# Dense blocks of U and V fetched in pairs by one engine, into a pool of their own

## The chip, the cores and the metric

The kernel runs on one core of a Trainium2 chip. The time is the device time of one execution in microseconds (us), and the kernel before stands at the median of three runs. Inside the core, TensorE (PE) multiplies matrices, VectorE (DVE) and ScalarE (ACT) work on rows of data, GpSimd (POOL) does some elementwise work and issues the indexed transfers, and SyncE (SP) issues plain transfers. Transfers between device memory and the on-chip memory are carried by 16 DMA engines, which all issuing engines share.

## The reference, cut to what matters

The program is one inference step of a decoder layer for 336 tokens (16 meta tokens, 256 of a prompt, 64 of running sequences). After convolution, state-space and output projections, every token passes an expert mixer with 16384 experts (PEER). That last part is where the change lies:

```python
q = (xb @ w_q).reshape(T, PEER_HEADS, 2, D_KEY // 2)
s = jnp.einsum('thcd,hckd->thck', q, keys)
s1, i1 = lax.top_k(s[:, :, 0], 16); s2, i2 = lax.top_k(s[:, :, 1], 16)
...
ids = i1 * N_KEYS + i2          # 8 heads x 16 experts per token, out of 16384
g = jax.nn.softmax(sc, axis=-1)
act = gelu(einsum('thkd,td->thk', U[ids], xb))
out = einsum('thk,thkd->td', g * act, V[ids])
```

U and V have 16384 rows of 1024 values each, 64 MB apiece.

## The kernel before, in words

The program is one function, `body`, with nested helpers. Tile's scheduler orders the instructions of each engine from priorities and a timeline of its own; PE's order in the first part is pinned.

**The first 530 us** are the projections, convolutions and state-space parts; weights come through `weight` (line 271) into the pool `wp` (line 290, tiles `wraw` x4, `wh` x2, `wl` x2, 4 KB per partition each).

**The query phase** (the loop over `j` at line 1180) multiplies by `w_q` and scores the keys. In it, `fetch` (line 1173) brings the first eight blocks of U into the pool `pre`.

**The dense phase** serves 184 tokens. U is read as 128 blocks of 128 experts, each block 128 partitions x 1024 floats, 4 KB per partition or 512 KB. `u_block` (line 1410) does 8 matmuls per block (each is two instructions in the trace, so 16 a block) into one of six PSUM tiles, and ACT evicts it with a Gelu into `S` (line 1417). Then V follows as 128 blocks in the same way: `v_block` (line 1514) multiplies `S` by the block into four running sums `va`. Between the blocks, 23 steps in each half (`g_step`, line 1423) build one-hot matrices `oh` on DVE, multiply them on PE into `pg` (line 1443), and scale `S` by the result on DVE (line 1454). So PE, which takes its instructions in order, waits at a step until DVE has built its `oh`.

**The gathered rows** serve the other 136 token columns: `gather` (line 1145) fetches 128 rows of U and V together (8 KB each, 1 MB in all) by an indexed transfer that POOL issues into one of five buffers `wuv`. Each gather is also made to wait for a block some steps back. `pick_dot` (line 1299) takes the products with the token on DVE (line 1303) and passes the sum through two activations on ACT (lines 1305 and 1308, tile `scg`); `pick_sum` (line 1310) adds the scaled V half on DVE (line 1313) and so frees the buffer. Here "row" means one such transfer of 128 rows. `Feed` (line 1350) deals these tasks, and the top-k tasks of the other tokens, out over the dense blocks. All of them go through in-order queues: DVE has top-k, rows and steps in one list, and ACT has evictions, `scg` activations and some transfers in one list.

**How dense blocks are brought**: `bring` (line 1380) issues transfers as long as the ring has room. `ring` (line 1368) hands out tiles `eraw` in the places of `wraw`, `wh` and `wl` of the pool `wp`, eight blocks in all, so block i reuses the place of block i-8. Blocks 8 to 15 take the ring, 16 to 23 go back into the `pre` places, and from 24 on the ring goes round. Line 1398 picks the issuing engine: odd blocks of V, and odd blocks of U after block 24, are issued from ACT, the others from SP. `extra_columns` (line 1287) sends four small transfers (`xigd`) through SP and later reads them back. `residual` reads the stored input `x1d` in two pieces, and `finish` (line 1490) normalizes the gathered tokens, with `fnorm` fetched by SP ahead of it, before `finish_dense` closes the program.

Of the kernel before, what the change touches and what calls it, by code (L numbers as in the profile page):

```python
# [7 lines left out]
F32 = mybir.dt.float32  # L8
# [9 lines left out]
D = 1024  # L18
KD = 8
# [22 lines left out]
ND = T2 - NGAT - NX  # L42
# [20 lines left out]
RB = 4  # L63
RING = RB + 4
LATE = 24
OH = 2
# [92 lines left out]
def body(tc, ia, oa, stop=None):  # L159
    nc = tc.nc  # L160
    with ExitStack() as top:
# [4 lines left out]
        x1d = dr.tile([128, KD, ND], F32, name="x1d")  # L166
        xs, xqs = ExitStack(), ExitStack()
        xq = xqs.enter_context(tc.tile_pool(name="xq", bufs=1, side=RIGHT))
# [120 lines left out]

        wp = top.enter_context(tc.tile_pool(name="wp", bufs=1))  # L290
        mix = top.enter_context(ExitStack())
# [878 lines left out]
        def place_of(n):  # L1170
            return pre_pools[n // PRE].tile([128, D], F32, name="pre", tag=f"pre{n}", bufs=1)

        def fetch(i):
            pre_pools.append(pres[i].enter_context(tc.tile_pool(name=f"pre{i}", bufs=1)))
            for n in range(PRE):
                u = place_of(len(fetched))
                nc.sync.dma_start(u, ia["uT"][len(fetched)])
                fetched.append(u.rearrange("p (k m) -> p k m", k=KD))

        for j in range(16):  # L1180
# [184 lines left out]

        nraw = [0]
# [6 lines left out]
        coming = ([("uT", b) for b in range(2 * PRE, 128)] + [("vE", b) for b in range(XRES)] + [("x1", 0), ("x1", 5)]  # L1373
                  + [("vE", b) for b in range(XRES, 128)])
        landed, turn = {}, [0]

        def again(name, i):
            return name == "uT" and 2 * PRE + RING <= i < AGAIN

        def bring():  # L1380
            while coming:
                name, i = coming[0]
                if again(name, i):
                    if len(ustep) <= i - 2 * PRE - RING:
                        return
                    raw = place_of(i - 2 * PRE - RING)
                else:
                    if turn[0] >= RING + used[0]:
                        return
                    raw = ring()  # L1390
                    turn[0] += 1
                coming.pop(0)
                if name == "x1":
                    n = min(5, KD - i)
                    raw = raw[:, :n * ND].rearrange("p (k t) -> p k t", t=ND)
                    nc.sync.dma_start(raw, x1d[:, i:i + n])
                else:
                    (nc.scalar if i % 2 and (name == "vE" or i > LATE) else nc.sync).dma_start(raw, ia[name][i])
                    raw = raw.rearrange("p (k m) -> p k m", k=KD)
                landed[name, i] = raw  # L1400

        used = [0]

        def block(name, i):
            bring()
            if not again(name, i):
                used[0] += 1
            return landed.pop((name, i))

        def u_block(b):  # L1410
            raw = fetched[b] if b < len(fetched) else block("uT", b)
            tag, nb = (("pj", 3), ("y", 2), ("pj", 3), ("y", 2), ("pj", 3), ("pb", 1))[b % 6]
            p = ps.tile([128, PJ], F32, name="pj", tag=tag, bufs=nb)[:, :T]
            for k in range(KD):
                i_ = nc.tensor.matmul(p[:, :ND], raw[:, k, :], nd[:, k, :], start=(k == 0), stop=(k == KD - 1))  # L1415
            ustep.append(i_.ins.name)
            nc.scalar.activation(Sv(b), p[:, :ND], AF.Gelu)  # L1417
# [62 lines left out]
        def residual():  # L1480
            xr = []
            for k0, n in ((0, 5), (5, 3)):
                r_ = block("x1", k0)
                xr += [r_[:, k] for k in range(n)]
            for k in range(KD):
                nc.tensor.matmul(va[k // 2][:, k % 2], ident, xr[k], start=False, stop=False, skip_group_check=True)
# [72 lines left out]
def layout(i):  # L1559
# [24 lines left out]
    def put(name, a):  # L1584
# [31 lines left out]
        peer_uv=np.concatenate([f["peer_u"][0], f["peer_v"][0]], 1),  # L1616
        uT=f["peer_u"][0].reshape(128, 128, 8, 128).transpose(0, 3, 2, 1).reshape(128, 128, D),
        vE=f["peer_v"][0].reshape(128, 128, D),
        fnorm=f["final_norm_w"],
# [33 lines left out]
```

## Time and profile before

| | |
|---|---|
| median of three runs | 1304.52 us (1301.46 to 1305.58) |
| the profiled execution | 1300.87 us, its span 1299.1 us |
| PE busy | 1270.9 us, 98% of the span |
| DVE, ACT, POOL busy | 74%, 41%, 46% |
| moved by the DMA engines | 373.80 MB |
| mean granted TensorE clock | 0.99 |

How to read the lines of the profile: a page shows one execution. Its slices divide the span into 40 equal parts; a digit is a busy share in tenths, and GB/s is what the DMA engines moved. Groups of instructions have line, engine, operation, `out<-in` by the program's tile names, a count, busy time and the mean of one; then the idle time ahead of them and what ended it. A timeline row has start, length, engine, line, operation, count, and in brackets the idle time before it with what released it. The table by windows has, for each stretch, the busy time of PE, PE's weight loads, DVE, ACT and POOL with their counts, then the granted clock, the DMA engines' busy share and GB/s. In the DMA answers, q0 is the queue of POOL's indexed transfers, q1 the queue of SP and q10 that of ACT.

### The profile page before, as it was taken

Reading aid. Unit: us, or ns where it says so; the run is one execution under the profiler, and the core shown is the slowest. Engines: PE = TensorE matmul, PEld = TensorE weight load, DVE = VectorE, ACT = ScalarE, POOL = GpSimd, SP = SyncE. Lnnn points to the kernel's source line nnn. Section 1 sums busy time; section 2 is a strip of 40 time slices with the busy share of each in tenths; the row PEclk is TensorE's granted clock in tenths of the full one; section 3 lists DMA queues with packets and bytes.
Section 4 is the critical chain, followed back from the end, with each engine's and each line's share of the span. In section 5 each row is a group of like instructions: output and inputs, shape, how many; then the busy total and the mean of one; then the engine's idle time right before and its main releaser. Section 6 shows DMA issues by size and latency. Waiting matters only on the chain.

```text
span 1299.1 us, 23902 instructions
## 1 busy us (share of the span) xinstructions
PE 1270.9 (98%) x9015; PEld 1223.2 (94%) x9015; DVE 956.2 (74%) x2240; ACT 529.6 (41%) x1395; POOL 592.9 (46%) x552
## 2 busy tenths in 40 slices
PE   9999999999989999999999899999999999999997
PEld 7998988999889999999999889999999999999997
DVE  7888778878887235549999968688788888545444
ACT  6787877888766444544232212212110110100102
POOL 2487777877774666974132223223332322122210
PEclk9899999999999999999999989999999999999999
DMA  6435453454433444766989999999999999999992
GB/s 246 165 126 185 155 191 134 156 186 167 149 129 136 146 149 153 254 231 221 382 328 416 416 414 415 414 412 408 413 414 415 415 415 414 402 414 415 405 414 88
DMA packets 85907, 373.80 MB, mean 288 GB/s; under 512 B 10000, under 2 KB 15376, under 8 KB 66208
## 3 DMA queue, kind: packets, MB, share of 16 engines
q1 hardware_dynamic: 48336, 166.82, 34.5%
q0 software_dynamic: 19584, 142.62, 26.9%
q10 hardware_dynamic: 17872, 62.84, 12.1%
q8 instruction: 71, 1.16, 0.4%
q14 instruction: 44, 0.36, 0.1%
HBM read 359.18 MB, written 13.06 MB: 287 GB/s over the span
## 4 chain that ended last, share of the span: by engine, by line
PE 83%; DVE 7%; DMA 6%; ACT 3%; issue 1%; POOL 1%; ACTq 0%; DVEq 0%
PE pj L176 32%; PE va L1517 25%; PE pj L1415 17%; DMA wuv<-in_peer_uv_dram,gid 3%; DMA eraw<-in_uT_dram 3%; PE pg L1443 1%; PE pst L176 1%; DVE ygat L1313 1%; PE po L176 1%; DVE wuv L1303 1%; PE pdec L176 1%; PE psc L1193 1%; PE py L176 1%; DVE pcv L509 1%; DMA wdt<-in_w_dt_dram 1%
## 5 line engine op out<-in xcount | busy, mean ns | idle before, releaser
L1147 POOL DMA_INDIRECT wuv<-in_peer_uv_dram,gid x136 | 173.0, 1272 | 484.7 <-PE va L1517 149.6
L247 POOL TENSOR_TENSOR wl<-wraw,wh 128x1024 fp32r<-128x1024 f32 (+1 forms) x160 | 279.6, 1760 | 117.1 <-ACT wh L243 68.8
L1517 PE MATMUL va<-S,eraw 128*128 128x184 f32 x2048 | 325.4, 320 | 0.0
L1517 PEld LDWEIGHTS va<-S,eraw 128*128 128x128 f32 x2048 | 318.9, 190 | 0.9 <-issue 0.9
L1415 PE MATMUL pj<-nd,eraw 128*128 128x184 f32 x1792 | 294.5, 324 | 9.9 <-DMA eraw<-in_uT_dram 8.1
L1415 PEld LDWEIGHTS pj<-nd,eraw 128*128 128x128 f32 x1792 | 282.8, 192 | 11.3 <-issue 9.0
L1313 DVE SCALAR_TENSOR_TENSOR ygat<-wuv,scg,ygat 128x1024 f32<-128x1024 f32 x128 | 164.1, 1282 | 108.1 <-ACT scg L1308 108.0
L176 PE MATMUL pj<-ah,wh 128*128 128x336 f32 (+1 forms) x768 | 242.5, 326 | 0.3 <-ACT xnf L219 0.3
L176 PE MATMUL pj<-al,wh 128*128 128x336 f32 (+1 forms) x768 | 232.2, 315 | 0.0
L1305 ACT ACTIVATE scg<-scg 128x1 f32<-128x1 f32 x136 | 27.3, 202 | 398.0 <-DVE wuv L1303 220.4
L1303 DVE SCALAR_TENSOR_TENSOR wuv<-wuv,x2m 128x1024 f32<-128x1024 f32 x128 | 156.2, 1220 | 17.3 <-DMA wuv<-in_peer_uv_dram,gid 17.0
L509 DVE SCALAR_TENSOR_TENSOR pcv<-ccat,vec,pcv 128x256 f32<-128x256 f32 x464 | 150.1, 389 | 17.1 <-ACT pcv L507 17.1
L243 ACT CAST wh<-wraw 128x1024 fp32r<-128x1024 f32 x125 | 131.2, 1050 | 73.4 <-PE pj L176 54.0
L176 PEld LDWEIGHTS pj<-ah,wh 128*128 128x128 f32 x768 | 145.4, 190 | 6.3 <-issue 2.0
L176 PEld LDWEIGHTS pj<-al,wh 128*128 128x128 f32 x768 | 145.0, 190 | 0.8
L176 PE MATMUL pj<-ah,wl 128*128 128x336 f32 (+1 forms) x768 | 137.2, 314 | 0.3 <-POOL wl L247 0.3
L176 PEld LDWEIGHTS pj<-ah,wl 128*128 128x128 f32 x768 | 119.8, 188 | 0.7 <-POOL wl L247 0.6
L1417 ACT ACTIVATE S<-pj 128x184 f32<-128x184 f32 x128 | 38.8, 318 | 128.0 <-PE pj L1415 127.7
L523 DVE SCALAR_TENSOR_TENSOR pj<-mcat,vec,pj 128x360 f32<-128x360 f32 x96 | 57.0, 595 | 0.6 <-ACT pj L521 0.6
L1454 DVE SCALAR_TENSOR_TENSOR S<-pg,S 128x232 f32<-128x232 f32 (+1 forms) x92 | 34.7, 420 | 29.8 <-PE pg L1443 29.6
L219 ACT ACT_TABLE_LOAD x38 | 48.8, 1283 | 0.7
L1415 PE MATMUL pj<-nd,pre 128*128 128x184 f32 x256 | 42.0, 319 | 0.0
(387 smaller groups left out, 1694.7 us busy)
## 6 DMA issues: line engine op xcount, KB each, us to landing
wraw<-in_w_in_dram SPq DMA_DIRECT2D x80, 512.0 KB, 3.3
eraw<-in_vE_dram SPq DMA_DIRECT2D x64, 512.0 KB, 9.5
eraw<-in_vE_dram ACTq DMA_DIRECT2D x64, 512.0 KB, 9.4
eraw<-in_uT_dram SPq DMA_DIRECT2D x60, 512.0 KB, 9.2
eraw<-in_uT_dram ACTq DMA_DIRECT2D x52, 512.0 KB, 9.9
st<-in_state_dram SPq DMA_DIRECT2D x8, 1024.0 KB, 6.9
out_ssm_s_dram<-st SPq DMA_DIRECT2D x8, 1024.0 KB, 6.3
wraw<-in_w_mo_dram SPq DMA_DIRECT2D x16, 512.0 KB, 3.2
```

The costliest lines, as they stand in the source:

```text
L176: i_ = nc.tensor.matmul(*a_, **kw)
L219: i_ = nc.scalar.activation(out, in_, f, **kw)
L243: (nc.vector.tensor_copy if on_dve else nc.scalar.copy)(h, src)
L247: (nc.gpsimd if on_pool else nc.vector).tensor_tensor(l[:, q:q + m], src[:, q:q + m], h[:, q:q + m].bitcast(F32), op=OP.subtract)
L509: t = nc.vector.scalar_tensor_tensor(o, i_, wv, a_, op0=OP.mult, op1=OP.add)
L523: nc.vector.scalar_tensor_tensor(o, cat[:, w:w + n], wv, o, op0=OP.mult, op1=OP.add)
L1147: i_ = nc.gpsimd.indirect_dma_start(out=u, out_offset=None, in_=ia["peer_uv"], in_offset=bass.IndirectOffsetOnAxis(ap=gid[:, c:c + 1], axi ...
L1303: nc.vector.scalar_tensor_tensor(u[:, :D], u[:, :D], 1.0, x2m if c < NPICK else x2e, op0=OP.mult, op1=OP.mult, accum_out=w)
L1313: nc.vector.scalar_tensor_tensor(a_, u[:, D:], scg[:, c:c + 1], a_, op0=OP.mult, op1=OP.add)
L1415: i_ = nc.tensor.matmul(p[:, :ND], raw[:, k, :], nd[:, k, :], start=(k == 0), stop=(k == KD - 1))
L1417: nc.scalar.activation(Sv(b), p[:, :ND], AF.Gelu)
L1517: i_ = nc.tensor.matmul(va[k // 2][:, k % 2], raw[:, k, :], Sv(b), start=(b == 0 and k % 2 == 0), stop=(b == 127), skip_group_check=True)
```

## The change

U and V are laid out in pairs of blocks: one transfer brings two blocks, 8 KB per partition, 1 MB. The ring becomes a pool `ep` of four pairs, still 32 KB per partition. It is opened on the right side of the on-chip memory after the query phase, in the place of `wp`, which is moved to the right side and closed there. A pair is free when its second block has been used. All pairs are issued by SP. The `pre` places hold pairs too, the input for `residual` comes in one piece, and the result of `finish` uses a place of `ep`.

```diff
-RING = RB + 4
-LATE = 24
+RING = 4
...
+        wp = wps.enter_context(tc.tile_pool(name="wp", bufs=1, side=RIGHT))
...
         xqs.close()
+        wps.close()
+        ep = top.enter_context(tc.tile_pool(name="ep", bufs=1, side=RIGHT))
...
         def ring():
-            tag, nb = (("wraw", rb[0]), ("wh", 2), ("wraw", rb[0]), ("wl", 2))[nraw[0] % 4]
-            nraw[0] += 1
-            return wp.tile([128, D], F32, name="eraw", tag=tag, bufs=nb)
+            return ep.tile([128, 2 * D], F32, name="eraw", bufs=RING)
...
-                    (nc.scalar if i % 2 and (name == "vE" or i > LATE) else nc.sync).dma_start(raw, ia[name][i])
-                    raw = raw.rearrange("p (k m) -> p k m", k=KD)
-                landed[name, i] = raw
+                    nc.sync.dma_start(raw, ia[name][n])
+                    raw = raw.rearrange("p (a k m) -> p a k m", a=2, k=KD)
+                landed[name, n] = raw
...
+        def block(name, b):
+            raw = pair(name, b // 2)[:, b % 2]
+            if b % 2 == 0:
+                bring()
+            elif not again(name, b // 2):
                 used[0] += 1
+            return raw
...
-            o = [wp.tile([128, D], F32, name="wraw", bufs=rb[0]) for _ in tiles]
+            o_ = ep.tile([128, 2, D], F32, name="o", tag="eraw", bufs=RING)
+            o = [o_[:, a] for a in range(n)]
...
+    def pairs(a):
+        return np.ascontiguousarray(a.reshape(64, 2, 128, D).transpose(0, 2, 1, 3).reshape(64, 128, 2 * D))
...
+        uT=pairs(f["peer_u"][0].reshape(128, 128, 8, 128).transpose(0, 3, 2, 1)),
+        vE=pairs(f["peer_v"][0]),
```

The scheduler writes some engines' lists anew. First SP, from the last `w_q` weights to the reading back of `xigd`. Before:

```order
L1398 DMA eraw<-in_uT_dram 128x1024 x8
L1398 DMA pre<-in_uT_dram 128x1024 x5
L1398 DMA eraw<-in_uT_dram 128x1024 x27
L1292 DMA xigd<-xig 8x8x8 x4
L1398 DMA eraw<-in_uT_dram 128x1024 x8
L1295 DMA xback<-xigd 128x16
```

And now:

```order
L1394 DMA eraw<-in_uT_dram 128x2048 x4
L1394 DMA pre<-in_uT_dram 128x2048 x4
L1394 DMA eraw<-in_uT_dram 128x2048 x26
L1293 DMA xigd<-xig 8x8x8
L1394 DMA eraw<-in_uT_dram 128x2048
L1293 DMA xigd<-xig 8x8x8 x3
L1394 DMA eraw<-in_uT_dram 128x2048 x7
L1296 DMA xback<-xigd 128x16
```

The first four ring transfers stood apart in time before, each behind the part of `wp` that it took over; now the first of them waits for the last use of the whole pool, and the other three follow at once. The small `xigd` transfers stand between pairs, and no dense transfer goes round them on another engine. At the end of the list three pairs stand behind the fetch of `fnorm`, where two single blocks stood.

Second ACT, about block 30 of U, where `scg` is a row's two activations and `S` a block's eviction. Before:

```order
L1417 ACTIVATE S_7584<-pj 128x184
L1398 DMA eraw<-in_uT_dram 128x1024
L1305 ACTIVATE scg<-scg 128x1
L1308 ACTIVATE scg<-scg,ggw 128x1
L1417 ACTIVATE S_7584<-pj 128x184
```

And now, in the same part:

```order
L1418 ACTIVATE S_8020<-pj 128x184 x2
L1306 ACTIVATE scg<-scg 128x1
L1309 ACTIVATE scg<-scg,ggw 128x1
L1418 ACTIVATE S_8020<-pj 128x184 x2
```

No transfer stands in ACT's list any more in the dense phase, and so none behind a row's activations. The place of the rows in the list moves as well. Counted in ACT's list, the rows that stand ahead of a block's eviction are, before and now: block 28 of U, 14 and 9; block 44, 23 and 19; block 72, 39 and 40; block 108, 59 and 61; block 124, 69 and 71.

Third DVE, ahead of the one-hot step that PE takes at block 108. Before, from one step's first matrix to the next:

```order
L1436 TENSOR_TENSOR oh<-iopw,i2T 128x1024
L1437 TENSOR_TENSOR oh<-iopw,i1T 128x512
L1313 SCALAR_TENSOR_TENSOR ygat<-wuv,scg,ygat 128x1024
L1439 TENSOR_TENSOR oh<-oh,gT 128x512 x2
L1303 SCALAR_TENSOR_TENSOR wuv,scg<-wuv,x2m 128x1024
```

And now:

```order
L1437 TENSOR_TENSOR oh<-iopw,i2T 128x1024
L1304 SCALAR_TENSOR_TENSOR wuv,scg<-wuv,x2m 128x1024
L1438 TENSOR_TENSOR oh<-iopw,i1T 128x512
L1440 TENSOR_TENSOR oh<-oh,gT 128x512 x2
L1314 SCALAR_TENSOR_TENSOR ygat<-wuv,scg,ygat 128x1024
L1304 SCALAR_TENSOR_TENSOR wuv,scg<-wuv,x2m 128x1024
L1314 SCALAR_TENSOR_TENSOR ygat<-wuv,scg,ygat 128x1024
L1304 SCALAR_TENSOR_TENSOR wuv,scg<-wuv,x2m 128x1024
L1314 SCALAR_TENSOR_TENSOR ygat<-wuv,scg,ygat 128x1024
L1304 SCALAR_TENSOR_TENSOR wuv,scg<-wuv,x2m 128x1024
L1314 SCALAR_TENSOR_TENSOR ygat<-wuv,scg,ygat 128x1024
```

The steps are the same, but at this place DVE takes four rows between two steps where it took one, so the rows are asked for earlier against the blocks.

More of the change, by code (lines that the diff above doesn't have):

```diff
@@ L166, in body @@
         x1d = dr.tile([128, KD, ND], F32, name="x1d")
-        xs, xqs = ExitStack(), ExitStack()
+        xs, xqs, wps = ExitStack(), ExitStack(), ExitStack()
+        wp = wps.enter_context(tc.tile_pool(name="wp", bufs=1, side=RIGHT))
         xq = xqs.enter_context(tc.tile_pool(name="xq", bufs=1, side=RIGHT))
@@ L1364, in drain, with again @@
                 self.tasks = []
-        nraw = [0]
         def ring():
-            tag, nb = (("wraw", rb[0]), ("wh", 2), ("wraw", rb[0]), ("wl", 2))[nraw[0] % 4]
-            nraw[0] += 1
-            return wp.tile([128, D], F32, name="eraw", tag=tag, bufs=nb)
[L1373 to L1378, printed above, removed]
+            return ep.tile([128, 2 * D], F32, name="eraw", bufs=RING)
+        coming = ([("uT", n) for n in range(PRE, 64)] + [("vE", n) for n in range(XRES // 2)] + [("x1", 0)]
+                  + [("vE", n) for n in range(XRES // 2, 64)])
+        landed, turn, used = {}, [0], [0]
+        def again(name, n):
+            return name == "uT" and PRE + RING <= n < AGAIN // 2
         def bring():
             while coming:
-                name, i = coming[0]
-                if again(name, i):
-                    if len(ustep) <= i - 2 * PRE - RING:
+                name, n = coming[0]
+                if again(name, n):
+                    if len(ustep) < 2 * (n - PRE - RING) + 2:
                         return
-                    raw = place_of(i - 2 * PRE - RING)
+                    raw = place_of(n - PRE - RING)
                 else:
@@ L1393, in bring, with pair @@
                 if name == "x1":
-                    n = min(5, KD - i)
-                    raw = raw[:, :n * ND].rearrange("p (k t) -> p k t", t=ND)
-                    nc.sync.dma_start(raw, x1d[:, i:i + n])
-                else:
-                    (nc.scalar if i % 2 and (name == "vE" or i > LATE) else nc.sync).dma_start(raw, ia[name][i])
-                    raw = raw.rearrange("p (k m) -> p k m", k=KD)
-                landed[name, i] = raw
[L1402 to L1406, printed above, removed]
+                    raw = raw[:, :KD * ND].rearrange("p (k t) -> p k t", t=ND)
+                    nc.sync.dma_start(raw, x1d)
+                else:
+                    nc.sync.dma_start(raw, ia[name][n])
+                    raw = raw.rearrange("p (a k m) -> p a k m", a=2, k=KD)
+                landed[name, n] = raw
+        def pair(name, n):
+            if (name, n) not in landed:
+                bring()
+            return landed[name, n]
+        def block(name, b):
+            raw = pair(name, b // 2)[:, b % 2]
+            if b % 2 == 0:
+                bring()
+            elif not again(name, b // 2):
                 used[0] += 1
-            return landed.pop((name, i))
+            return raw
         def u_block(b):
-            raw = fetched[b] if b < len(fetched) else block("uT", b)
+            raw = fetched[b // 2][:, b % 2] if b < 2 * PRE else block("uT", b)
             tag, nb = (("pj", 3), ("y", 2), ("pj", 3), ("y", 2), ("pj", 3), ("pb", 1))[b % 6]
@@ L1480, in residual @@
         def residual():
[L1481 to L1484, printed above, removed]
+            xr = pair("x1", 0)
+            used[0] += 1
             for k in range(KD):
-                nc.tensor.matmul(va[k // 2][:, k % 2], ident, xr[k], start=False, stop=False, skip_group_check=True)
+                nc.tensor.matmul(va[k // 2][:, k % 2], ident, xr[:, k], start=False, stop=False, skip_group_check=True)
         fin = []
```

9 lines of the change are left out of this document (3 added, 6 removed).

## The prediction, made before the changed kernel was run

> **What bounds the kernel now.** I read the page's chain of waits first, then a table by windows over the dense phase, then PE's timeline where that table shows PE short of busy. The page gives the chain by engine, and what the DMA engines moved in each fortieth of the span:
>
> ```profile
> GB/s 246 165 126 185 155 191 134 156 186 167 149 129 136 146 149 153 254 231 221 382 328 416 416 414 415 414 412 408 413 414 415 415 415 414 402 414 415 405 414 88
> ...
> PE 83%; DVE 7%; DMA 6%; ACT 3%; issue 1%; POOL 1%; ACTq 0%; DVEq 0%
> ```
>
> PE carries the time, but from the middle of the span on the DMA engines stand at about 415 GB/s in nearly every slice. The windows tell which of the two ends last, stage by stage:
>
> ```profile
> 685.00:726.00 41.00, 41.00 (x264) 40.68 (x263) 39.20 (x115) 11.04 (x34) 9.12 (x9) 1.00 1.02 415
> 726.00:779.00 53.00, 45.98 (x284) 44.76 (x282) 39.59 (x82) 12.04 (x47) 13.78 (x12) 0.90 1.02 416
> 779.00:820.00 41.00, 38.13 (x299) 37.36 (x297) 34.78 (x58) 8.69 (x32) 12.18 (x9) 1.00 1.02 416
> 820.00:950.00 130.00, 129.80 (x1045) 127.93 (x1044) 105.21 (x191) 27.53 (x100) 39.79 (x27) 1.00 1.02 412
> 950.00:1118.00 168.00, 168.00 (x1365) 166.59 (x1364) 136.65 (x237) 18.22 (x73) 46.07 (x35) 1.00 1.02 415
> 1118.00:1210.00 92.00, 92.00 (x592) 92.00 (x591) 44.65 (x56) 8.95 (x36) 19.22 (x18) 1.00 1.02 410
> ```
>
> PE is short only between 726 and 820 us, in the U half; over the V half (950 on) it is busy throughout, so nothing in V's transfers can shorten V. The DMA engines' share is 1.02 in all six rows: there is no idle transfer time in the whole stretch. PE's timeline names the losses:
>
> ```profile
> 730.04 5.25 PE L1415 MATMUL pj<-nd,eraw 128*128 128x184 f32 x32 [1.82 <-ACT S L1417]
> 737.40 9.40 PE L1415 MATMUL pj<-nd,eraw 128*128 128x184 f32 x48 [2.10 <-DMA eraw<-in_uT_dram]
> ...
> 773.02 5.25 PE L1415 MATMUL pj<-nd,eraw 128*128 128x184 f32 x16 [3.09 <-DMA eraw<-in_uT_dram]
> ...
> 784.50 7.72 PE L1415 MATMUL pj<-nd,eraw 128*128 128x184 f32 x48
> ...
> 814.54 2.73 PE L1415 MATMUL pj<-nd,eraw 128*128 128x184 f32 x16 [2.87 <-DMA eraw<-in_uT_dram]
> ```
>
> The four waits are 1.82 + 2.10 + 3.09 + 2.87 = 9.88 us. After two of them the granted clock falls (the 0.90 above): 48 instructions take 9.40 us where 48 elsewhere take 7.72, and 16 take 5.25 where 16 take 2.73, so 1.68 + 2.52 = 4.20 more. All that can be won is 14.08 us.
>
> **Why PE waited.** ACT's timeline ahead of the waits, with its own transfers (ACTq) between its work:
>
> ```profile
> 716.91 0.33 ACTq L1398 DMA_DIRECT2D eraw<-in_uT_dram  x1
> ...
> 723.18 0.20 ACT L1305 ACTIVATE scg<-scg 128x1 f32<-128x1 f32 x1 [5.56 <-DVE wuv L1303]
> ...
> 728.02 0.33 ACTq L1398 DMA_DIRECT2D eraw<-in_uT_dram  x1
> ...
> 748.69 0.34 ACTq L1398 DMA_DIRECT2D eraw<-in_uT_dram  x1
> ...
> 762.43 0.20 ACT L1305 ACTIVATE scg<-scg 128x1 f32<-128x1 f32 x1 [4.53 <-DVE wuv L1303]
> 762.44 0.33 ACTq L1398 DMA_DIRECT2D eraw<-in_uT_dram  x1
> ```
>
> ACT's issues stand 11.1 and 13.8 us apart where two blocks take about 5.1 (7.72 us is three blocks): they sit in the list behind a row's activation that waits for DVE. The DMA answers show what this does to the shares. With both dense queues filled (690 to 726 us), and then with one of them only (744 to 748 us):
>
> ```profile
> q0 software_dynamic: 1025, 7.48, 50.6%
> q1 hardware_dynamic: 1015, 3.70, 25.7%
> q10 hardware_dynamic: 1021, 3.70, 25.4%
> ...
> eraw<-in_uT_dram SPq DMA_DIRECT2D x7, 512.0 KB, 10.6
> ```
>
> ```profile
> q0 software_dynamic: 154, 1.11, 66.6%
> q10 hardware_dynamic: 147, 0.54, 33.4%
> ```
>
> The packet counts of the first are equal: the engines give each queue one packet in turn, 8 KB to a row and 4 KB to a block. Two dense queues get half, one gets a third. So a late ACT issue also hands the engines to the rows.
>
> **The change part by part.** *ACT's issues go.* The waits at 737 and 773 us have this cause: 2.10 + 1.68 + 3.09 + 2.52 = 9.39 us. The 1.82 at 730 is an eviction behind a row; the new list has 19 rows ahead of block 44's eviction where there were 23, so I count it as gone too. Upper end 11.21 us. ACT's own saved issue time is worth nothing (ACT is busy 12.04 of 53 us).
>
> *One queue with 8 KB packets.* Against the rows it has turns of equal size: half, as two queues had, and whenever SP has a pair in hand. Neutral while both queues were filled.
>
> *Larger packets.* The page has the cost of both sizes, q0 all rows, q10 mostly blocks:
>
> ```profile
> DMA packets 85907, 373.80 MB, mean 288 GB/s; under 512 B 10000, under 2 KB 15376, under 8 KB 66208
> ...
> q0 software_dynamic: 19584, 142.62, 26.9%
> q10 hardware_dynamic: 17872, 62.84, 12.1%
> ```
>
> Per MB that is 0.269 x 16 x 1299.1 / 142.62 = 39.2 engine-us against 0.121 x 16 x 1299.1 / 62.84 = 40.0: 2% less on the dense half, 1% of the whole, 2.6 us of the 265 from 685 to 950. The Trainium skill ("DMA: Bandwidth & Descriptors", "Anatomy of one DMA") gives a DMA about 2.0 us plus its bytes at 436 GB/s. By that, an estimate, two single blocks cost 6.4 us and a pair 4.4, the engines would cease to bind and the sum would be the upper end. The trace disagrees: with several transfers in flight 415 GB/s were reached with single blocks, so that fixed part is already covered.
>
> *Coarser ring.* A pair is issued when four pairs back is done and needed three pairs later, 6 x 2.57 = 15.4 us. Bounds for its landing: 6.9 us alone, and 16.0 for the median row, of which up to five wait in one queue.
>
> ```profile
> st<-in_state_dram SPq DMA_DIRECT2D x8, 1024.0 KB, 6.9
> ```
>
> I take the 10.6 us above: there too a block was served at 5.05 us (a quarter of 415 GB/s) and a pair at half is the same 5.05. Cover 4.8 us, cost 0; at 16 us it would be 0.6 us per pair.
>
> *xigd.* From 786 to 812 us, blocks behind these small transfers on SP, and on ACT beside them, landed in
>
> ```profile
> eraw<-in_uT_dram SPq DMA_DIRECT2D x5, 512.0 KB, 22.2
> eraw<-in_uT_dram ACTq DMA_DIRECT2D x5, 512.0 KB, 10.6
> ```
>
> SP loses 11.6 us, a turn for each small packet. Now all blocks stand behind them, but a round has one other queue (8 KB) and not two (12 KB): 11.6 x 2/3 = 7.7, less the cover of 4.8 leaves 2.9 us. So the 2.87 at 814 stays.
>
> *Pool behind the query phase.* The ring's first transfers wait for PE's last use of `wp`, which ends just before the first row here; the second row is where the ring's first block is used:
>
> ```profile
> 604.90 0.61 PE L1193 MATMUL psc<-keys,qT 128*128 128x128 f32 x4
> ...
> 619.15 0.79 PE L1415 MATMUL pj<-nd,eraw 128*128 128x184 f32 x4
> ```
>
> 14.2 us for a pair at 10.6: cost 0. The next pairs follow at 5.05 us each and are needed at about 5.1.
>
> *End.* Three pairs stand behind `fnorm` on SP:
>
> ```profile
> 1255.93 0.33 SPq L992 DMA_DIRECT2D wuv<-in_fnorm_dram  x1
> 1260.24 5.31 SPq L1398 DMA_DIRECT2D eraw<-in_vE_dram  x2
> ```
>
> The first of these pairs can be issued when all but 12 blocks are done, about 1257 us, later than 1255.93; cost 0 while rows are not over 5 us late.
>
> *What the engines take back.* With a share of 1.02 up to 950 us and beyond, PE can be at V 11.2 us sooner only if 11.2 x 415 = 4.6 MB are moved sooner or left for later. Cheaper packets give 2.6 us. Rows can be late by what they land early: the median from issue to landing in 690 to 850 and in 850 to 950 us is
>
> ```profile
> q0 software_dynamic: 5012, 36.48, 55.3%
> ...
> wuv<-in_peer_uv_dram,gid POOLq DMA_INDIRECT x34, 16.0
> ```
>
> ```profile
> wuv<-in_peer_uv_dram,gid POOLq DMA_INDIRECT x21, 11.4
> ```
>
> so 4.6 us. But the new order asks for rows earlier late in U: 61 for 59 ahead of block 108's eviction, 71 for 69 at 124; two rows of 1.05 MB are 5.1 us. That leaves 2.6 + 4.6 - 5.1 = 2.1 us as the lower end. Between 2.1 and 11.2 I take 5.0, nearer to the lower end because of the 1.02, and above it because early in U the order asks for fewer rows (9 for 14 at block 28), which frees DVE's early time.
>
> The sum: 1300.87 - 5.0 = 1295.9 us for a profiled execution like this one. The median of the runs shown is 3.65 us above it; from the median, 1304.5 - 5.0 = 1299.5 us.
>
> **The rivals.** *All waits go* (chance 0.18): rows prove less pressing than counted, and PE runs through U. 11.2 us, up to 14.1 with `xigd`: about 1292. For it: the chain to the waits went through ACT. Against: the 1.02.
>
> *The engines bind wholly* (0.20): the waits reappear as PE waiting at `pg` for `oh` or at an eviction. 2.1 us less, or nothing: 1303.
>
> *Rows become late* (0.20), slower. In 690 to 850 us rows had 55.3% of queue time; a punctual dense queue holds them to 50. Then 34 rows become 30.7, 3.3 rows late at 160 / 34 = 4.7 us, 15.5 us. Less the 4.6 they can bear, 10.9; about half of it falls on PE, since a PE that waits fills its ring and then leaves the engines to the rows: 5.5 us slower, 1310. It decides from about 7 us of lateness on, at the steps about block 72 to 110, where DVE takes up to four rows ahead of one `oh`. For it: the new DVE list there. Against: PE's lost time no longer feeds back through ACT's issues.
>
> *One queue gets a third* (0.04): pairs are cut into 4 KB turns, so the change does not do what it says. Dense blocks would get 138 GB/s beside five queued rows, 3.8 us a block; each such spell would cost PE what it lost at 737 and 773 us, and it would come oftener: 6 us slower, 1310. Against: 85907 - 66208 = 19699 packets of 8 KB or more are over 2000 more than the 17408 of 136 rows, so SP's transfers with 8 KB per partition, as `st`, go in whole packets. The Trainium skill ("DMA: Bandwidth & Descriptors", "SWDGE vs HWDGE vs iDMA") states a packet of preferably at most 4096 B as the boundary at which an engine changes queues. By that rule this case holds; the counts here say otherwise.
>
> **How the numbers follow.** The forecast has 0.38 and 1299.5 us. A measurement of this kernel tells 0.3%, 3.9 us, from no change. Faster by more: all of the first rival, most of the forecast's case (0.27), 0.02 of the second: 0.47. Within: 0.10 of the forecast's, 0.15 of the second, 0.03 of the third: 0.28. Slower: 0.25, the rest. The range reaches from 1290 (every wait gone) to 1311 (rows late, with 1 us of spread).
>
> **What would show it.** Right: no wait for `eraw` at PE about blocks 50 to 66, all dense traffic on q1 at near half of the engines' time with packets of 8 KB, the share still 1.02, a wait about block 78 behind `xigd`, V begun about 5 us sooner and unchanged in length. Wrong: a share clearly under 1 between 685 and 950 us (first rival), PE waiting for DVE's `oh` by more than 5 us in sum (second or third), or pairs landing after 15 us away from `xigd`.

## The result, and the profile after

The changed kernel takes 1312.19 us (median of 10 runs, 1308.13 to 1314.76), the kernel before 1304.44 us (10 runs, 1301.46 to 1306.61): a ratio of 1.0058, interval 1.0043 to 1.0072, 7.6 us slower. The profiled execution took 1310.24 us, 9.37 more than the one before the change, its span 1308.5 us.

The page's chain of waits, by engine: PE has lost share, DVE has gained.

```profile
PE 71%; DVE 17%; DMA 6%; ACT 3%; issue 2%; POOL 1%; ACTq 0%; DVEq 0%
```

The table by windows for the stretches that the prediction showed:

```profile
685.00:726.00 41.00, 38.46 (x248) 38.17 (x248) 39.82 (x110) 12.70 (x37) 15.12 (x10) 1.00 1.01 412
726.00:779.00 53.00, 49.47 (x326) 48.86 (x326) 35.34 (x51) 10.16 (x44) 14.94 (x13) 0.97 1.01 419
779.00:820.00 41.00, 35.47 (x259) 34.79 (x258) 31.31 (x52) 7.33 (x32) 12.15 (x10) 0.92 1.01 419
820.00:950.00 130.00, 126.47 (x1025) 125.03 (x1024) 114.38 (x204) 27.32 (x107) 38.36 (x28) 0.99 1.01 416
```

The DMA engines are as full as they were (share 1.01). From 685 to 950 us together they moved 416 GB/s where it was 414: if the larger packets did that, they are worth 0.5%, half of what was taken. PE's timeline has the losses, and they are others:

```profile
719.63 20.21 PE L1416 MATMUL pj<-nd,eraw 128*128 128x184 f32 x128 [2.54 <-ACT S L1418]
...
743.37 6.67 PE L1416 MATMUL pj<-nd,eraw 128*128 128x184 f32 x32 [3.53 <-ACT S L1418]
...
791.70 8.08 PE L1416 MATMUL pj<-nd,eraw 128*128 128x184 f32 x32 [4.94 <-ACT S L1418]
...
811.34 0.76 PE L1444 MATMUL pg<-oh 128*128 128x64 f16 x10 [0.46 <-DVE oh L1440]
...
852.35 1.29 PE L1444 MATMUL pg<-oh 128*128 128x64 f16 x16 [3.39 <-DVE oh L1440]
```

PE no longer waits for a dense block. It waits 14.86 us for evictions and one-hot matrices that stand in ACT's and DVE's lists behind rows, where it waited 9.88 us before. ACT's timeline ahead of the first of these waits shows the order: the row's activation waits for DVE, and the two evictions come right behind it.

```profile
718.84 0.20 ACT L1306 ACTIVATE scg<-scg 128x1 f32<-128x1 f32 x1 [4.34 <-DVE wuv L1304]
719.08 0.29 ACT L1309 ACTIVATE scg<-scg,ggw 128x1 f32<-128x1 f32 x1
719.28 0.52 ACT L1418 ACTIVATE S<-pj 128x184 f32<-128x184 f32 x2
```

Four points of the timeline tell where the 9.37 us come in: the ring's first product (619.15 before), V's first product and the first product of the final normalization, after and then before:

```profile
620.74 0.79 PE L1416 MATMUL pj<-nd,eraw 128*128 128x184 f32 x4
...
957.47 3.00 PE L1517 MATMUL va<-S,eraw 128*128 128x184 f32 x16
...
1294.43 2.63 PE L1530 MATMUL prd<-sqd,cst 128*128 128x184 f32 x14
```

```profile
950.80 2.71 PE L1517 MATMUL va<-S,eraw 128*128 128x184 f32 x16
...
1287.47 2.63 PE L1530 MATMUL prd<-sqd,cst 128*128 128x184 f32 x14
```

Ahead of the ring's first product 1.6 us are lost, in U 5.1 (336.7 for 331.7), in V 0.3, behind V 2.4 (14.1 for 11.6 to the span's end): 9.4 us.

**The 1.6 us** are scatter. In eleven experiments, kernels of both kinds, that product falls between 618.7 and 622.2 us. So from here on the *dense stage* is counted from it to the first `prd` product: 668.3 us before, 673.7 after. (Some expectations below count from block 12, 11.0 us later: 657.3 and 662.6.)

**The 2.4 us behind V** are two table loads of ACT in the last chain:

```profile
1280.46 1.28 ACT L1501 ACT_TABLE_LOAD   x1
1281.75 1.28 ACT L1306 ACT_TABLE_LOAD   x1
...
1298.33 1.28 ACT L219 ACT_TABLE_LOAD   x1 [1.10 <-DVE rsv L233]
1299.63 0.36 ACT L219 ACTIVATE rst<-rsv 128x184 f32<-128x184 f32 x1
1300.00 1.28 ACT L219 ACT_TABLE_LOAD   x1
```

The scheduler now puts the preload for the normalization (L1501) ahead of the last row's Gelu (L1306), which loads its own table over it. Each later function then loads a table again. Before, the preload stood behind the last row and the chain had no load. The Trainium skill ("ScalarE: Activation LUTs", "What ACT_TABLE_LOAD costs") gives a switch 1.28 us and a drain of 1.38 us more. The load agrees; the drain does not show here, since the next activation starts 0.02 us after the load.

**The 5.1 us in U.** What the DMA engines did between 560 and 605 us, before and after:

```profile
DMA packets 2183, 8.00 MB, mean 178 GB/s; under 512 B 240, under 2 KB 240, under 8 KB 2177
...
eraw<-in_uT_dram SPq DMA_DIRECT2D x7, 512.0 KB, 3.2
wraw<-in_w_q_dram SPq DMA_DIRECT2D x5, 512.0 KB, 3.3
pre<-in_uT_dram SPq DMA_DIRECT2D x3, 512.0 KB, 5.1
```

```profile
DMA packets 1027, 3.85 MB, mean 86 GB/s; under 512 B 120, under 2 KB 120, under 8 KB 997
...
wraw<-in_w_q_dram SPq DMA_DIRECT2D x5, 512.0 KB, 3.9
```

The parts of `wp` used to come free one at a time, and ten blocks were issued in these 45 us, while the engines were half idle. The new pool opens when all of `wp` is done, and its first pair is issued at 606.78: 4.15 MB are missing by then. PE does not notice, as the ring is used only from 620.74 on. But the first rows now share the engines with the whole ring: row 5, counted from 0, has its last packet at 648.7 us for 642.3. The scheduler's lists also put the early rows off (9 for 14 at block 28). The bytes moved in the 165 us that end 65.85 us behind the ring's first product, before and after:

```profile
520.00:685.00 165.00, 164.74 (x1111) 163.50 (x1110) 131.07 (x522) 64.78 (x174) 85.75 (x99) 1.00 0.77 286
```

```profile
521.59:686.59 165.00, 164.74 (x1110) 163.43 (x1109) 129.93 (x553) 64.64 (x168) 78.18 (x94) 1.00 0.69 270
```

16 GB/s over 165 us: 2.6 MB are still missing (the rates are whole GB/s, so this and the table's MB are good to about 0.15). What is missing there is rows, not blocks. The queues in the same two stretches, before and after:

```profile
q1 hardware_dynamic: 7963, 26.49, 43.9%
q0 software_dynamic: 2365, 17.28, 27.4%
q10 hardware_dynamic: 859, 3.14, 4.9%
```

```profile
q1 hardware_dynamic: 6233, 30.57, 47.9%
q0 software_dynamic: 1891, 13.79, 20.6%
```

SP and ACT had moved 26.49 + 3.14 = 29.63 MB, now SP alone 30.57: the blocks have caught up. The rows are 3.49 MB behind. Two things hold them back. The engines are full from 635 to 655 us (share 1.01 and 1.02 in the two halves), and DVE's list has top-k work ahead of the rows: row 5 is taken 5.6 us after its landing before the change (647.91), and 12.8 us after it now, with DVE busy in between. So buffers come free later, and the engines even have time left then:

```profile
661.48 1.22 DVE L1304 SCALAR_TENSOR_TENSOR wuv<-wuv,x2m 128x1024 f32<-128x1024 f32 x1
```

```profile
665.00:675.00 10.00, 10.00 (x67) 10.00 (x66) 9.90 (x17) 1.84 (x8) 2.78 (x3) 1.00 0.71 270
```

From 685 us to V the engines are full, and 2.6 MB at 415 GB/s are 6.4 us. This is the theory that the experiments test: **a debt of early transfers**, carried through a stretch in which the engines have nothing to spare. Its rivals are the queues' shares (one queue with 8 KB packets holds the rows to half) and the rows' places in the lists.

### The profile page after: what moved, and what is told of

The parts are those of the page before. It is cut to its first block, busy times and chain, and to the rows that moved or that the text cites. A ratio compares the mean times of both kernels' runs of the same rounds, so it can differ in the third digit from the quotient of the medians.

```text
span 1308.5 us, 23635 instructions
## 1 busy us (share of the span) xinstructions
PE 1271.7 (97%) x9015; PEld 1224.8 (94%) x9015; DVE 959.9 (73%) x2240; ACT 532.1 (41%) x1400; POOL 597.6 (46%) x552
## 4 chain that ended last, share of the span: by engine, by line
PE 71%; DVE 17%; DMA 6%; ACT 3%; issue 2%; POOL 1%; ACTq 0%; DVEq 0%
PE pj L176 31%; PE va L1517 24%; PE pj L1416 7%; DMA wuv<-in_peer_uv_dram,gid 5%; DVE ygat L1314 3%; DVE wuv L1304 3%; PE pg L1444 1%; PE pst L176 1%; PE po L176 1%; PE pdec L176 1%; PE py L176 1%; DVE pcv L508 1%; ACT L219 1%; DVE S L1455 1%; DMA wdt<-in_w_dt_dram 1%
## 5 line engine op out<-in xcount | busy, mean ns | idle before, releaser
L1146 POOL DMA_INDIRECT wuv<-in_peer_uv_dram,gid x136 | 179.3, 1318 | 483.6 <-PE va L1517 164.6
L1306 ACT ACTIVATE scg<-scg 128x1 f32<-128x1 f32 x136 | 27.6, 203 | 472.6 <-DVE wuv L1304 472.5
## 6 DMA issues: line engine op xcount, KB each, us to landing
eraw<-in_uT_dram SPq DMA_DIRECT2D x56, 1024.0 KB, 10.2
```

Of the source, the lines that this page charges most:

```text
L1146: i_ = nc.gpsimd.indirect_dma_start(out=u, out_offset=None, in_=ia["peer_uv"], in_offset=bass.IndirectOffsetOnAxis(ap=gid[:, c:c + 1], axi ...
```

## The experiments

All numbers in one table. The ratio is to executions of the kernel before on the same chip; the medians come from several chips, so runs are compared by their ratios. The dense stage is that of one profiled execution. "Missing" is the difference in MB to the kernel before in those 165 us.

| run | median us | ratio (95%) | dense stage us | missing MB |
|---|---|---|---|---|
| before | 1304.44 | 1 | 668.3 | 0 |
| after | 1312.19 | 1.0058 (1.0043 to 1.0072) | 673.7 | 2.6 |
| e1_tail | 1310.65 | 1.0044 (1.0028 to 1.0061) | 676.0 | 2.6 |
| e2_late | 1306.70 | 1.0016 (1.0001 to 1.0031) | 673.6 | 3.1 |
| e3_sp | 1302.30 | 0.9987 (0.9972 to 1.0002) | 668.3 | -0.5 |
| e4_raw | 1308.41 | 1.0040 (1.0025 to 1.0054) | 676.4 | 1.8 |
| e5_early | 1307.29 | 1.0015 (1.0004 to 1.0026) | 673.3 | 1.5 |
| e6_skip | 1307.55 | 1.0017 (1.0004 to 1.0031) | 675.1 | - |
| e7_rows | 1309.27 | 1.0029 (1.0018 to 1.0041) | 675.4 | 2.5 |
| e8_split | 1313.21 | 1.0059 (1.0044 to 1.0075) | 677.5 | 3.0 |
| e9_mix | 1307.38 | 1.0020 (1.0010 to 1.0030) | 674.1 | 2.0 |
| e10_splate | 1308.98 | 1.0038 (1.0023 to 1.0053) | 675.2 | 2.5 |
| e11_act | 1314.08 | 1.0077 (1.0064 to 1.0090) | 677.6 | 3.1 |

**e1_tail: the table loads alone.**

```diff
+                after(pl, gelus[-1])
                 tc.keep_in_program_order(pl)
```

> The changed kernel, with one more order: ACT's preload of the table for the final normalization stands behind the last row's Gelu (L1306), not ahead of it. Nothing else moves in ACT's list of rows. Theory: the two table loads of 1.28 us at 1298.33 and 1300.00 in the last chain are there only because the preload was undone by the last row; both go, 2.4 to 2.6 us less than the changed kernel, about 1309.7 us, and the stretch from V's last product to the end is 11.6 us again as before the change. Rival: the end is later because the result of finish waited for a place of ep until 1279.7; then the loads go from the list but the time stays at 1312 us.

The last chain of its profile has no load:

```profile
1284.11 1.28 ACT L1504 ACT_TABLE_LOAD   x1
...
1301.91 0.36 ACT L219 ACTIVATE rst<-rsv 128x184 f32<-128x184 f32 x1 [1.11 <-DVE rsv L233]
1302.30 0.36 ACT L219 ACTIVATE rst<-rst 128x184 f32<-128x184 f32 x1
```

From the first `prd` product to the span's end it takes 11.5 us, as before the change: the loads were the 2.4 us. The ratio falls by 0.0014, 1.8 us, which the ratios alone could not tell from nothing. Its dense stage is 2.3 us longer than that of the changed kernel, which has the same transfers: so much two profiled executions can differ.

**e2_late: the debt alone, in the kernel before.**

```diff
+                    if name == "uT" and i < 24:
+                        tc.add_manual_dep(i_.ins, held, ...)
```

> The kernel before, with one thing added: blocks 8 to 23 of U wait for the last product with w_q, so nothing of the ring is brought ahead of about 605 us; single blocks, 4 KB packets, ACT and SP both issue. Theory of the debt (the changed kernel brought 4.15 MB less ahead of 605 us, and engines that are full from 685 us on carry that as lateness until V): the same 4 MB are missing here; the order asks for two rows fewer in U (68 for 70 ahead of the last eviction, 2.1 MB), so V begins (4.15 - 2.1) / 0.413 = 5.0 us later, and 1 to 4 us of that may be made good between 605 and 685 us where the share was 0.92: 1306 to 1309 us. Rival, the queue's share (one queue of 8 KB packets holds the rows to half): two queues are kept here, so no change, 1304.4 us. Rival, the order of the rows (few early, more of them in the middle of U): the early part is as in the changed kernel (9 for 14 rows at block 28), the middle is not (35 for 39 at block 72), so PE's waits behind rows at blocks 40 to 70 do not come and the time is 1304 us or less.

The dense stage grows by 5.3 us, with two queues, single blocks and 4 KB packets: neither one queue nor larger packets are needed for such a loss. It is paid in V (346.6 for 336.7 us), since the list leaves two rows more to V. By the ratio the kernel is only 2 us slower, its interval reaching down to nearly nothing. So a cleaner pair was wanted, and came with e10_splate.

**e3_sp: the issuing engine alone, in the kernel before.**

```diff
-                    (nc.scalar if i % 2 and (name == "vE" or i > LATE) else nc.sync).dma_start(raw, ia[name][i])
+                    nc.sync.dma_start(raw, ia[name][i])
```

> The kernel before, with all dense blocks issued by SP: single blocks, packets of 4 KB, one queue; the rows keep their places in U's list (70 ahead of the last eviction, 39 at block 72). If the engines give each queue one packet in turn, the dense queue has 4 of every 12 KB while rows are queued, 138 GB/s or 3.8 us a block for 2.57: PE waits for eraw over most of U, 6 us slower or more, 1310 us up, and rows land early. If the share were by bytes or the engines' total alone decided, the late issues of ACT go and nothing else changes: 1300 us. The theory of the debt says nothing of it: what is brought ahead of 605 us is as before.

Neither number came. The turns are as expected: from 690 to 726 us the dense queue gets a third, packet for packet with the rows,

```profile
q0 software_dynamic: 1343, 9.77, 65.7%
q1 hardware_dynamic: 1421, 5.18, 35.9%
```

and blocks come 3.78 us apart, each with a wait of about 1 us:

```profile
718.21 2.73 PE L1415 MATMUL pj<-nd,eraw 128*128 128x184 f32 x16 [1.05 <-ACT scg L1308]
721.99 2.73 PE L1415 MATMUL pj<-nd,eraw 128*128 128x184 f32 x16 [1.05 <-DMA eraw<-in_uT_dram]
725.77 2.73 PE L1415 MATMUL pj<-nd,eraw 128*128 128x184 f32 x16 [1.04 <-DMA eraw<-in_uT_dram]
```

But PE's waits for `eraw` in U sum to 9.1 us, where the three long ones of the kernel before made 8.1, and the dense stage is the same to 0.1 us. Taking ACT's late issues away did not bring the 9.4 us of the prediction: the wait only stands elsewhere. The edit also takes one of the two dense queues away, so what the late issues cost at an unchanged share is not shown. The rows' larger share early on brings them no more in the end: from 690 to 850 us they move 36.48 MB, as before. The gain of 1.7 us lies within the interval.

**e4_raw: two of four pairs brought early again.**

```diff
+        w4 = wr.tile([128, 4, KD, 128], F32, name="w4")
...
+            if n % 4 < 2:
+                return w4[:, 2 * (n % 2):2 * (n % 2) + 2].rearrange("p a k m -> p (a k m)")
```

> The changed kernel with two of the four pairs of the ring in the place of wraw alone, which stays open, so that they can be brought from about 585 us on, ahead of the end of the query phase; the other two keep the new pool. The result of finish uses a wraw place, and the preload stands behind the last row as in the run beside it. Theory of the debt: 2 pairs, 2.1 MB or 5.0 us of the engines' time, are back; the order has as many rows in U (73), so V begins about 5 us sooner than in the changed kernel, and with the 2.4 us of the end 1304.7 us. If the lateness came from one queue with 8 KB packets, or from the rows' order in the middle of U (40 at block 72 here too), the two early pairs change nothing: 1309.7 us as the run with the end alone.

The median is 3.7 us above the 1304.7 expected, no better than e1_tail within the intervals. The theory in its first form fell here: of 2.1 MB brought back by 605 us only 0.8 are left 65.85 us behind the ring's first product (1.8 missing for 2.6). When the ring is full early, it stops asking, and in the last 80 us of that stretch the engines' share is 0.91 where the changed kernel has 0.94. On this reading, what counts is what is missing when the engines become full for good, at about 685 us. Besides, V's start lost 5.5 us in waits for `S` here, which nothing in the theory foretold.

**e5_early: all four pairs early, two of them in row buffers.**

```diff
+                for _ in range(2):
+                    u = gp.tile([128, 2 * D], F32, name="wuv", bufs=UV)
+                    nc.sync.dma_start(u, ia["uT"][PRE + len(late)])
```

> The changed kernel with four pairs again brought ahead of the end of the query phase: two in the place of wraw as in the run before, and two more (blocks 8 to 11) in two of the five row buffers, which are idle until 607 us. The preload stands behind the last row. Theory of the debt: 102 MB are moved by 605 us as before the change (the changed kernel: 97.8), the rows keep nearly the old places early (13 for 14 at block 28), and the dense stage (block 12 to the end of V) falls from 662.6 us to 657 to 659, less 1 to 3 us if the larger packets are worth their 1%; the median is at most 1 us above that of the kernel before. Rival, the list at the seam of U and V (73 rows ahead of the last eviction, where the run with two pairs early lost 5.5 us in waits for S and their clock): the gain of U is lost at V's start and the median stays 4 to 6 us above. Rival, one queue with 8 KB packets: as the run with the end alone, 5.7 us above.

It is 3.8 us better than e1_tail by the ratios (0.0029, the intervals apart), and 2 us worse than before, where at most 1 was expected. The dense stage misses its 657 to 659 us: counted from block 12 it takes 662.3. The share from 605 to 685 us says why not all came back:

```profile
605.00:685.00 80.00, 80.00 (x525) 80.00 (x524) 76.92 (x322) 22.84 (x77) 19.88 (x17) 1.00 0.85 336
```

0.85 for 0.92: rows with three buffers for five could not use the time. 1.5 MB stay missing, 3.6 us; the dense stage is 5.0 us over that before. Early transfers and early rows (13 for 14) come back together here, so the run does not tell them apart.

**e6_skip: 3.15 MB less to move.**

```diff
+                if skip(name, n):
+                    coming.pop(0)
+                    landed[name, n] = landed[name, n - 1]
+                    continue
```

> The changed kernel with the preload behind the last row, and with three pairs of U left out (pairs 14, 16 and 18: their six blocks multiply the pair ahead of them once more), so 3.15 MB less from about 660 to 690 us; every product, eviction, step and row is still done. If the bytes that the engines have to move from 605 us on set the time, the dense stage is 3.15 / 0.415 = 7.6 us shorter than the 662.6 to 664.9 us of the two runs with the same transfers: 655 to 658 us, and the median 2 us under to 1 us over that of the kernel before. If the places of the rows in DVE's and ACT's lists set it (DVE too slow between steps), the bytes change nothing: 5.7 us above the kernel before, with the waits at PE's evictions as they were.

It is 3.5 us better than e1_tail by the ratios, whose intervals just meet; that is half of what the bytes are worth. The profiled dense stage takes 664.1 us from block 12, where 655 to 658 were expected. PE's timeline shows where it was stopped:

```profile
839.20 1.29 PE L1456 MATMUL pg<-oh 128*128 128x64 f16 x16 [9.28 <-DVE oh L1452]
```

PE was ahead at its blocks (block 84 began at 824.7 us, 832.8 in the changed kernel) and then waited 9.28 us at the next step, whose one-hot stands in DVE's list behind rows that were still on their way. So bytes are not the whole of it: a list that ties blocks to rows passes on a gain only as far as the rows have it too. (A wait of 8.17 us for a one-hot stands at 855.28 us in e1_tail as well.)

**e7_rows: three rows moved from U to V.**

```diff
-NU = (45, 26, 35)
+NU = (45, 23, 38)
```

> The changed kernel with the preload behind the last row, and three rows fewer dealt to the second part of U and three more to V (26, 35 become 23, 38): 70 rows ahead of the last eviction as before the change, for 73. If U's order alone is at fault, U is 3 x 1.05 / 0.415 = 7.6 us shorter, V is as it was (336.9 us) and the median is 2 us under the kernel before. If the engines bind over U and V together, what U gains V pays: U shorter by 5 to 8 us, V longer by as much, the median 4 to 6 us above the kernel before.

Neither. U is not shorter (338.7 us from the ring's first product to V's first, 336.7 in the changed kernel) and V not longer (336.7). All waits in U lie ahead of block 92, and up to there the list is unchanged. The 2 us by the ratio lie within the intervals. It is no test of the theory.

**e8_split: the pool and the one queue, with 4 KB packets.**

```diff
-                    nc.sync.dma_start(raw, ia[name][n])
+                    for a in range(2):
+                        nc.sync.dma_start(raw[:, a * D:(a + 1) * D], ia[name][n][:, a * D:(a + 1) * D])
```

> The changed kernel with the preload behind the last row, each pair brought as two transfers of 512 KB on SP: the pool and the single queue stay, the packets are 4 KB again. The order asks for two rows fewer at the last eviction (71 for 73) and three at block 72. If turns of 4 KB against the rows' 8 KB starve the dense queue, PE waits for eraw in U and the time is 5 us or more above the run with the end alone. If the engines' total decides, only the packets' cost changes, 1 to 2% of the dense half (415 for 419 GB/s, 1% of 525 us at most, 2 to 5 us), less what two rows moved out of U give: within 3 us of the run with the end alone, 1306 to 1312 us.

It is 2 us over e1_tail, within both intervals. PE's waits in U change sides: 16.1 us for `eraw` and 1.0 for evictions, where e1_tail has 17.0 for evictions and one-hots. In this pair the queue with the larger share decides who is late, not by how much.

**e9_mix: the ring back in the places of the query phase.**

```diff
+            if n % 2 == 0:
+                return w4[:, n % 4:n % 4 + 2].rearrange("p a k m -> p (a k m)")
+            return [wp.tile([128, D], F32, name="eraw", tag=("wh", "wl")[n % 4 // 2], bufs=2) for _ in range(2)]
```

> The changed kernel with the ring back in the places of the query phase: pairs 4, 6, 8 and so on go as one transfer into two places of wraw, the others as two transfers of 512 KB into the places of wh and of wl; all from SP, no row buffer is used for U, and the preload stands behind the last row. So the early transfers of the kernel before are back without the loss of row buffers that the run with four early pairs had (share 0.85 from 605 to 685 us there). Theory of the debt: about 102 MB by 605 us, 130 to 131 by 685 us (block 12 at 630 us as origin), the dense stage 656 to 659 us, the median between 2 us under and 1.5 us over the kernel before. If single issue, the larger pieces or the rows' list cost time of their own (73 rows ahead of the last eviction here too), it stays 3 to 6 us over the kernel before.

By the ratio it is 3 us better than e1_tail and 2.6 worse than before, where at most 1.5 was expected. A pair needs two `wraw` places at once, so only part comes early: 2.0 MB are missing, 4.8 us at 415 GB/s, and the dense stage is 5.8 us longer. The expected 102 MB by 605 us were not reached, so this is no full undoing of the debt either.

**e10_splate: the debt alone, against e3_sp.** The edit of e2_late on top of that of e3_sp.

> The kernel before with all dense blocks issued by SP, as in the third run, and with blocks 8 to 23 of U held until the last product with w_q, as in the second. Against the third run (dense stage 657.2 us, 0.9987 of the kernel before) only the early transfers differ, and ACT issues nothing in either. Theory of the debt: 97.8 MB at 605 us for 102.5, 127.5 to 128 MB at 685 us for 131, the dense stage 4 to 6 us longer, 661 to 663 us, the ratio to the kernel before 1.002 to 1.004. If early transfers are worth nothing (the loss belonging to pairs, pool or packets), the dense stage stays at 657 us and the ratio at 0.999.

The pair differs by one edit, and ACT issues no dense block in either. The lists that the scheduler writes differ with it: in ACT's trace 9 rows for 14 stand ahead of block 28's eviction, and 69 for 70 ahead of the last. The bytes in the 165 us, e3_sp and then e10_splate:

```profile
523.07:688.07 165.00, 164.74 (x1111) 163.50 (x1110) 131.13 (x522) 64.52 (x174) 85.96 (x99) 1.00 0.77 289
```

```profile
520.48:685.48 165.00, 164.74 (x1111) 163.50 (x1110) 130.38 (x551) 63.83 (x167) 80.14 (x94) 1.00 0.71 271
```

18 GB/s are 3.0 MB, 7.2 us at 415 GB/s. Again it is rows that are missing, e3_sp and then e10_splate:

```profile
q0 software_dynamic: 2371, 17.33, 27.0%
```

```profile
q0 software_dynamic: 1894, 13.81, 20.6%
```

The dense stage goes from 668.3 to 675.2 us, 6.9 more, nearly all of it in V (345.3 for 338.9 us). The ratio goes from 0.9987 to 1.0038, 6.6 us, with the intervals well apart. PE waits in many pieces of about 1 us, in U and now in V also (5.3 us for `eraw` there). So the late opening of the ring, together with the lists that the scheduler writes for it, is worth 6.6 us, without pairs, pool or 8 KB packets. No run opens the ring late and keeps the old place of the rows. How much of the 6.6 us comes from the crowded engines and how much from rows that the list takes later therefore stays open.

**e11_act: pairs issued from both engines.**

```diff
-                    nc.sync.dma_start(raw, ia[name][n])
+                    (nc.scalar if n % 2 and (name == "vE" or n > 12) else nc.sync).dma_start(raw, ia[name][n])
```

> The changed kernel with the preload behind the last row, and with odd pairs issued by ACT as odd blocks were before (all of V, of U from pair 13 on). Two queues of 8 KB packets against the rows' one: while all three are filled the rows have a third. If the engines' total sets the time, nothing changes against the run with the end alone (5.7 us over the kernel before, within 2 us). If the rows' share decides, rows come later and PE waits longer at evictions and steps: 3 us or more on top of it. If ACT's late issues cost what the prediction gave them (9.4 us in U), waits for eraw come back and it is 5 us or more on top.

It is 4.3 us over e1_tail, the intervals apart. Waits for `eraw` come back (11.0 us in U), the longest

```profile
770.51 21.86 PE L1419 MATMUL pj<-nd,eraw 128*128 128x184 f32 x128 [3.62 <-DMA eraw<-in_uT_dram]
```

So with pairs, issuing from SP alone is the better choice. The rows' share did not fall to a third: from 690 to 726 us they have 58.1%, where e1_tail has 51.2%, so the dense queues were not always filled. That fits pairs that are issued late, but 0.5 MB more are missing as well (3.1 for 2.6): how the 4.3 us divide stays open.

**Together.** Four ratios lead from the kernel before to the changed one: all on SP 0.9987 (1.7 us less, within the interval), the ring late 1.0038 (6.6 us more), pairs in the new pool 1.0044 (0.8 more, within it), the table loads 1.0058 (1.8 more, within it too). Missing MB at 2.41 us each are near most of the dense stages' excess over that before: e5_early 3.6 us for 5.0 measured, e9_mix 4.8 for 5.8, the changed kernel 6.4 for 5.4 and 7.7 in e1_tail, e10_splate 6.0 for 6.9, e8_split 7.2 for 9.2, e11_act 7.6 for 9.2. Two stand out: e4_raw (4.4 for 8.1, with its loss at V's start) and e2_late (7.6 for 5.3, with two rows fewer in U). e4_raw's loss at V's start was not followed up, and stays open. These excesses lean on one execution of the kernel before, which is 3.6 us under its median. By the ratios most are smaller: 2.0 us for e5_early, 2.6 for e9_mix, 5.7 for e1_tail, 5.0 for e10_splate, 7.7 for e8_split, 5.2 for e4_raw, 3.8 for e7_rows (6.0 by its bytes) and 2.1 for e2_late, but 10.0 for e11_act. So the bytes give the size of the loss, within 2 us in five of these nine, and not its order. No version beat the kernel before by more than its interval; e3_sp is the best of them.

## Why the prediction was wrong, point by point

- **Pool behind the query phase, "cost 0": the step that failed.** It was priced by PE alone: 14.2 us from the pool's opening to its first use, cover for one pair. Right for PE, which waits for nothing there. But the prediction itself had shown that the engines are full from 685 us on, and there transfers not made early are owed. The shortfall measured 4.15 MB at 605 us, 2.6 MB at about 685 us, 6.4 us by the rate and 6.6 by e10_splate; in the changed kernel's own U half 5.1 us are lost.
- **"ACT's issues go", 9.39 us: the term that was mis-sized.** e3_sp takes those issues away, and one dense queue with them, and gains 1.7 us, not to be told from nothing. The sign was right (no long wait for `eraw`), but the second rival's reason, that waits reappear elsewhere while the share is 1.02, held almost wholly. The 1.82 us at an eviction, counted as gone too, did not go: PE now waits 11.0 us at evictions.
- **Fewer rows early (9 for 14 at block 28), taken as a point for the gain**: it is where the debt stands, 3.49 MB of rows at 686.59 us. A row put off in a stretch with room is a row to be moved in a stretch without. Whether the list only follows the late ring or adds to its cost is not shown.
- **The table loads, 2.4 us**, were not in the sum. They stand in the order of ACT's list at its end, which the prediction did not go into.
- **`xigd`, 2.87 us, was said to stay**: it went. The only wait from 800 to 820 us is 0.46 us, for a one-hot.
- **Right**: one queue gets half (1081 packets of rows to 965 on SP from 690 to 726 us, 53.1% to 47.7%); pairs land after 10.2 us in U for 10.6 taken (below); the share stays at 1.01; V is unchanged in length (337.0 for 336.7 us). The larger packets give 0.5% for the 1% taken. The section of the Trainium skill that the prediction names there, "Anatomy of one DMA", has its figure for transfers that GpSimd issues; the pairs are issued by SP, and the sum did not use it.
- **The rivals.** "Rows become late" named the sign, and its 1310 us is within 2.2 of the median, by luck. Its place (from about block 72) and its mechanism were others: three of the five waits come ahead of 800 us, and the rows were not held to half. From 690 to 850 us they had 58.0% of the time (below). They were late because they began late and were taken late. The sign named for it, more than 5 us of waits for `oh`, did not come either (3.85 us). "One queue gets a third" is excluded by the packet counts above.

The page's row on U's pairs in the changed kernel (count, KB, median us to landing), and the rows' queue from 690 to 850 us:

```profile
eraw<-in_uT_dram SPq DMA_DIRECT2D x56, 1024.0 KB, 10.2
```

```profile
q0 software_dynamic: 5272, 38.44, 58.0%
```

With the debt (6.4) and the loads (2.4) and nothing for ACT's issues, the sum would have been 1300.87 + 8.8 = 1309.7 us for the profiled execution, which took 1310.24. That is reckoned after the fact, and its parts do not fit as well as the total: U lost 5.1 us and not 6.4, and 1.6 us are scatter.

## What to carry to other kernels

Where a later stretch has no idle transfer time, price a delayed prefetch by its bytes, not by whether its first user waits: count what is missing at the moment the engines become full, and divide by their rate there. Ask also whose bytes these are: here the delayed blocks had caught up, and the debt stood in other transfers, which the new lists had put off. In these runs a wait that vanished in such a stretch mostly came back elsewhere, and leaving bytes out brought half of their price. And a buffer whose parts come free one by one is itself a prefetch: merging the parts, or the pool around them, gives that up.

## What the hardware showed

- A turn of the engines was a packet, whether of 4 or of 8 KB: 4 KB against 8 KB gave 1421 packets to 1343 (e3_sp), 8 KB against 8 KB 965 to 1081:

```profile
q0 software_dynamic: 1081, 7.93, 53.1%
q1 hardware_dynamic: 965, 6.98, 47.7%
```

  The Trainium skill ("DMA: Bandwidth & Descriptors", "Queues, rings and completion order") says that each engine takes turns between its queues at the grain of packets. These counts agree.
- Many short waits left the clock alone where few long ones did not. In e3_sp nine waits for `eraw` of at most 1.12 us stand in the U half and the granted clock is 1.00 in every window of it. In the kernel before, waits of 1.82, 2.10 and 3.09 us stand in the window with 0.90. A long wait does not always do it: behind the 2.54 us at 719.63 in the changed kernel, 128 instructions run at full rate, and behind the 2.87 us at 814.54 in the kernel before, 16 do.
